# A macaron decoder layer: four instead of three of eight pairs by seven products in every other block of the gate and up groups

## Chip, core and metric

The kernel runs on one core of one Trainium2 chip. The metric is the device time of one execution in microseconds (us). Matrix products run on TensorE (PE), elementwise work on VectorE (DVE) and ScalarE (ACT), and loads of weights are issued on the queue of SyncE (SP).

## What is computed

One decoder layer on an input of 256 rows and 2048 columns: a half feed-forward network (FFN1), three gated token mixers, and a second half feed-forward network (FFN2). The change touches only the first product of the two FFNs:

```python
def swiglu_half_ffn(x, norm_g, w_gate_up, w_down):
    h = rmsnorm(x, norm_g)
    gate, up = jnp.split(h @ w_gate_up, 2, axis=-1)
    return 0.5 * ((jax.nn.silu(gate) * up) @ w_down)
```

`w_gate_up` has 2048 rows and 2 x 5632 columns, all in float32.

## The kernel before

**Precision.** A float32 operand is split into a high part that PE takes (`h`, `wh`) and the low rest (`l`, `wl`). A product is then three matmuls: high x high, low x high, high x low (`add_product`, L241). The split of a weight tile is called a cut (`cut`, L236): ACT copies the high part, DVE subtracts it from the raw weights to give the low part.

**Tiles.** The input is transposed once into eight pages, each with two k-tiles of 128 rows, both parts, and both row tiles (`t` = 0, 1). A pair `u` is two k-tiles, so there are eight pairs. The gate and up columns are worked off in eleven blocks of 512 columns (`NFC`). Block 0 goes through `mm_group`. Blocks 1 to 10 go through `pair_group` (L248), which computes 512 gate columns and 512 up columns for both row tiles at once: a 2 x 2 block of outputs (row tile `t`, half `n`).

**Two kinds of pair.** For each pair `pair_group` loads two 512 KB pieces of weights into a `raw` buffer (there are three). An ordinary pair has eight products: four outputs by two k-tiles, 24 matmuls with 128 x 512 outputs. Its cuts are two of 1024 elements per partition. A seven-product pair takes the 2 x 2 by 2 x 2 block product with seven multiplications (the scheme of Strassen and Winograd), 21 matmuls. For it the left side needs four combinations of the input, which `form_page` (L215) makes once per pair and FFN and keeps in a page of `forms`. The weights need combinations too, made anew in every block on DVE: `ta` (L290), `tb` (L295, L296), with a cut of each (`hal`, `hbl` are the low parts) beside a plain cut of 1024 and one of 512 elements. Its seven products go to three of the four output accumulators and to four intermediate ones, `p1`, `p5`, `p6`, `p7`. Each accumulator is one of the eight PSUM banks. After the last seven-product pair of a block, ACT copies `p1` and DVE makes four combinations of the intermediates (L314 to L318, tiles `ua`, `u`, `uv`). At the end of the block `ffn` adds them to the four accumulators (L471), and `gated` (L447) applies the gate (L453 on ACT, L455 on DVE).

**Order.** The order of pairs in a block is `MIXED`, (3, 0, 4, 1, 5, 2, 6, 7), and pairs 0, 1 and 2 are the seven-product ones, at the second, fourth and sixth place. `pair_group` takes its `seven` from the pages in `forms` unless it is given; `form_steps` makes three. The same function with the same order serves other weights (L595, L903, L925). The down product (L505, L511) uses it with orders of its own; in its second call five seven-product pairs alternate with ordinary ones.

**Side steps.** A queue `side` holds small steps that `tick` runs between matmuls. `pair_group` ticks twice in every ordinary pair that comes after the last seven-product pair of its block (L282), so four times in a block. `put` (L417) is two steps: each transposes half of the block's hidden values on PE, and the second one also writes them to DRAM on SP's queue (L431). The last block also takes `get` steps for the down product.

**Buffers and scheduling.** Cut weights have five buffers for each part (`wh`, `wl`). `ta`, `tb` and the parts of their cuts lie in a pool of 30 pages, which also holds the input's pages and the forms. A scheduler fixes the order of each engine's instructions when the kernel is built, and puts in the waits; loads on SP's queue are issued in that order.

Of the kernel before, what the change touches and what calls it, by code (L numbers as in the profile page):

```python
# [21 lines left out]
FF = 5632  # L22
NFC = FF // 512
DOWN = (2, 5, 8, 11, 14)
MIXED = (3, 0, 4, 1, 5, 2, 6, 7)
KF = FF // P
EPS = 1e-6
# [6 lines left out]
def hybrid_layer(  # L34
# [37 lines left out]
    side = deque()  # L72
# [139 lines left out]
    def lhs_of(tiles):  # L212
        return lambda k, part, t: tiles[k // 2][:, k % 2, part, t * P : (t + 1) * P]

    def form_page(forms, tiles, j):  # L215

        xp = tiles[j]
        v, f = temp([2, S], "fv"), temp([4, P], "ff")
        nc.vector.tensor_tensor(v, xp[:, :, 0, :].bitcast(F32), xp[:, :, 1, :].bitcast(F32), ALU.add)
        a12, a22, a11, a21 = (v[:, kk, t * P : (t + 1) * P] for kk in range(2) for t in range(T))  # L220
        nc.vector.tensor_tensor(f[:, 0, :], a21, a22, ALU.subtract)
        nc.vector.tensor_tensor(f[:, 1, :], f[:, 0, :], a11, ALU.subtract)
        nc.vector.tensor_tensor(f[:, 2, :], a11, a21, ALU.subtract)
        nc.vector.tensor_tensor(f[:, 3, :], f[:, 1, :], a12, ALU.add)
        dst = page([2, 4, P], F32R, "form")
        nc.scalar.activation(dst[:, 0, :, :], f, AF.Copy)
        nc.vector.tensor_tensor(dst[:, 1, :, :], f, dst[:, 0, :, :].bitcast(F32), ALU.subtract)
        forms[j] = dst
# [180 lines left out]
    def form_steps(forms, tiles, n=3):  # L409
        return [lambda j=j: form_page(forms, tiles, j) for j in range(n)]  # L410

    def ffn(lx, forms, rs, wgu, wd, stream, cb, before=None):
        hid, flat = [], {}
        hdram = dp.tile([NFC - 1, P, 4 * S], F32, tag="hd", name="hd", bufs=2)
        rh = st.tile([P, T], F32, tag="rh", name="rh")
# [1 line left out]
        def put(c, hd):  # L417

            dst = []

            def turn(jj):
                if jj == 0:
                    dst.append(page([4, S], F32, "hf"))
                ps = aux([2, S], "hid")
                for j in range(2):
                    for t in range(T):
                        k = 2 * jj + j
                        nc.tensor.transpose(ps[:, j, t * P : (t + 1) * P], hd[t][:, k * P : (k + 1) * P], ident)  # L428
                nc.scalar.activation(dst[0][:, 2 * jj : 2 * jj + 2, :], ps, AF.Copy)
                if jj == 1:  # L430
                    nc.sync.dma_start(out=hdram[c], in_=dst[0].rearrange("p k s -> p (k s)"))  # L431

            return [lambda: turn(0), lambda: turn(1)]
# [30 lines left out]
        for c in range(1, NFC):  # L464
            if c == NFC - 1:
                side.extend(put_last)
            acc, terms = pair_group(wgu, c * 512, FF + c * 512, lx, forms, MIXED)
            for n in range(2):
                for t in range(T):
                    d = terms[t, n]  # L470
                    nc.vector.tensor_tensor(d, acc[t, n], d, ALU.add)  # L471
            hd = gated(c, [terms[t, 0] for t in range(T)], [terms[t, 1] for t in range(T)])
            if c < NFC - 1:
                side.extend(put(c, hd))
            if c == NFC - 2:
                put_last = [lambda: get(0), lambda: get(1)]
        drain()
# [27 lines left out]
        ps, terms = pair_group(wd, 0, 512, lh, down, range(KF // 2), DOWN, first_block)  # L505
# [5 lines left out]
        ps, terms = pair_group(wd, 1024, 1536, lh, down, order, DOWN, second_block)  # L511
# [34 lines left out]
    forms0 = {}  # L546
# [3 lines left out]
    s0 = Stream([xv[:, :, c * 512 : (c + 1) * 512] for c in range(4)])  # L550
    cb, x1, rs, s1 = residual(s0, G_MIX, "x1")
    lx = lhs_of(x1)
    ffn(lhs_of(tiles0), forms0, rs0, ffn1_w_gate_up[0], ffn1_w_down[0], s0, cb, before=before)


    def head_norm(buf, nh, name):
# [378 lines left out]
        for t in range(T):  # L935
            nc.sync.dma_start(out=out[0, t * P : (t + 1) * P, c * 512 : (c + 1) * 512], in_=o[:, t, :])

    ffn(lhs_of(x2), forms2, rs, ffn2_w_gate_up[0], ffn2_w_down[0], s2, store)


# [30 lines left out]
```

## Time and profile before

| | us |
|---|---|
| median of 3 runs | 2128.67 (2128.15 to 2128.83) |
| profiled execution | 2128.03 |
| its span, first to last instruction | 2126.30 |
| PE busy | 2114.2 (99%) |
| DVE busy | 1739.4 (82%) |
| ACT busy | 1186.1 (56%) |

The span runs from the first instruction to the last on the core; the execution's time has some start and end around it. Blocks 1 to 10 of FFN1 lie between about 57 and 482 us of the span, those of FFN2 between about 1464 and 1889 us. Block 4 of FFN1 begins on PE at about 184.2 us and block 5 at 226.65 us. Ends of matmuls are modelled, so the start of one to the start of the next tells what it costs. The rows of DVE and ACT overlap with their neighbours by some hundredths to a tenth of a microsecond, so there too the distance of starts is the cost, where no idle time is noted.

### The profile page before, as it was taken

To read this page: it belongs to the slowest core of one execution; us is meant where nothing else is said; L and a number is where in the kernel's file an instruction comes from. 1 tells how busy PE (TensorE), PEld (TensorE's weight loads), DVE (VectorE), ACT (ScalarE), POOL (GpSimd) and SP (SyncE) were. 2 spreads that over 40 slices of the span, in tenths; PEclk is the share of its full clock that TensorE was granted. 3 is DMA by queue.
4 is the path that set the end of the run, shared out by engine and by line. 5 is a ranking of instruction groups with operands and counts; after the bars stand their busy time and mean duration, and the time that the engine had idled before them with its cause. 6 is when DMAs were issued, how large, how long until landed. Compare 5 with 4: busy or idle time off the path is not lost.

```text
span 2126.3 us, 26105 instructions
## 1 busy us (share of the span) xinstructions
PE 2114.2 (99%) x9683; PEld 1744.7 (82%) x9683; DVE 1739.4 (82%) x2221; ACT 1186.1 (56%) x1488; POOL 3.5 (0%) x24
## 2 busy tenths in 40 slices
PE   9999999999999999999999999999999999999999
PEld 7888888888888888887788888878888888888887
DVE  7898899889858788657669878898899889989675
ACT  6555555556545565555655555565555555556453
POOL 0000000000000000000000000000000000000000
PEclk9999999999999999999999999999999999999999
DMA  7666666666866654754456656575666666677764
GB/s 260 206 213 212 207 210 216 211 230 223 274 211 205 225 204 149 250 165 157 139 178 217 198 189 211 195 250 199 214 217 207 209 208 218 208 235 245 258 193 148
DMA packets 221508, 444.67 MB, mean 209 GB/s; under 512 B 12654, under 2 KB 13764, under 8 KB 221380
## 3 DMA queue, kind: packets, MB, share of 16 engines
q1 hardware_dynamic: 221088, 442.96, 62.7%
q8 instruction: 76, 1.25, 0.2%
q14 instruction: 52, 0.43, 0.1%
q10 hardware_dynamic: 292, 0.05, 0.0%
HBM read 426.16 MB, written 16.79 MB: 208 GB/s over the span
## 4 chain that ended last, share of the span: by engine, by line
PE 97%; DVE 1%; DMA 1%; ACT 0%; issue 0%; SPq 0%; ACTq 0%; DVEq 0%
PE mm L244 74%; PE mm L352 20%; PE hid L428 1%; DMA raw<-in_ffn_w_gate_up_dram 1%; DVE wl L346 0%; PE x L200 0%; DVE xr L389 0%; PE fpt L851 0%; PE fav L861 0%; PE mg L200 0%; PE flg L823 0%; PE mlg L729 0%; PE mav L756 0%; PE flg L821 0%; ACT wh L345 0%
## 5 line engine op out<-in xcount | busy, mean ns | idle before, releaser
L238 ACT ACTIVATE wh<-raw 128x1024 fp32r<-128x1024 f32 x608 | 599.7, 988 | 634.6 <-PE mm L244 362.5
L239 DVE TENSOR_TENSOR wl<-raw,wh 128x1024 fp32r<-128x1024 f32 x608 | 682.4, 1132 | 204.6 <-ACT wh L238 203.8
L244 PE MATMUL mm<-wh,x 128*128 128x512 f32 x2300 | 713.5, 391 | 0.0
L244 PEld LDWEIGHTS mm<-wh,x 128*128 128x128 f32 x2300 | 428.7, 188 | 87.3
L244 PE MATMUL mm<-wl,x 128*128 128x512 f32 x1150 | 446.7, 390 | 0.0
L244 PE MATMUL mm<-wh,hid 128*128 128x512 f32 x1168 | 357.7, 390 | 0.0
L352 PE MATMUL mm<-wh,x 128*128 128x512 f32 (+1 forms) x960 | 291.7, 382 | 2.9 <-ACT x L189 2.8
L346 DVE TENSOR_TENSOR wl<-raw,wh 128x1024 fp32r<-128x1024 f32 (+2 forms) x170 | 196.8, 1161 | 95.8 <-ACT wh L345 94.9
L345 ACT ACTIVATE wh<-raw 128x1024 fp32r<-128x1024 f32 (+2 forms) x170 | 170.5, 1009 | 169.7 <-PE mm L352 97.3
L244 PEld LDWEIGHTS mm<-wh,hid 128*128 128x128 f32 x1168 | 218.8, 188 | 45.1
L244 PEld LDWEIGHTS mm<-wl,x 128*128 128x128 f32 x1150 | 215.9, 188 | 45.3
L244 PE MATMUL mm<-wl,hid 128*128 128x512 f32 x584 | 222.4, 389 | 0.0
L352 PEld LDWEIGHTS mm<-wh,x 128*128 128x128 f32 x960 | 175.6, 188 | 38.6 <-ACT x L189 4.2
L352 PE MATMUL mm<-wl,x 128*128 128x512 f32 (+1 forms) x480 | 181.4, 379 | 0.2 <-DVE wl L346 0.2
L290 DVE TENSOR_TENSOR ta<-raw 128x1024 f32<-128x1024 f32 x101 | 123.1, 1219 | 12.0 <-DMA raw<-in_ffn_w_gate_up_dram 6.4
L244 PEld LDWEIGHTS mm<-wl,hid 128*128 128x128 f32 x584 | 109.6, 188 | 22.8
L239 DVE TENSOR_TENSOR hbl<-tb,hbh 128x1024 fp32r<-128x1024 f32 x101 | 123.2, 1220 | 2.5 <-ACT hbh L238 2.3
L239 DVE TENSOR_TENSOR hal<-ta,hah 128x1024 fp32r<-128x1024 f32 x101 | 123.2, 1220 | 1.4 <-ACT hah L238 1.4
L238 ACT ACTIVATE hbh<-tb 128x1024 fp32r<-128x1024 f32 x101 | 106.3, 1053 | 30.1 <-DVE tb L296 30.0
L238 ACT ACTIVATE hah<-ta 128x1024 fp32r<-128x1024 f32 x101 | 106.3, 1052 | 27.5 <-DVE ta L290 27.1
L244 PE MATMUL mm<-hah,form 128*128 128x512 f32 x404 | 121.5, 389 | 0.0
L352 PEld LDWEIGHTS mm<-wl,x 128*128 128x128 f32 x480 | 90.1, 188 | 16.3 <-DVE wl L346 0.6
(318 smaller groups left out, 2198.2 us busy)
## 6 DMA issues: line engine op xcount, KB each, us to landing
raw<-in_ffn_w_gate_up_dram SPq DMA_DIRECT2D x322, 512.0 KB, 4.5
raw<-in_ffn_w_down_dram SPq DMA_DIRECT2D x176, 512.0 KB, 5.1
raw<-in_w_in_dram SPq DMA_DIRECT2D x80, 512.0 KB, 5.1
raw<-in_w_in_dram SPq DMA_DIRECT2D x36, 1024.0 KB, 5.0
raw<-in_w_out_dram SPq DMA_DIRECT2D x32, 512.0 KB, 5.1
raw<-in_ffn_w_gate_up_dram SPq DMA_DIRECT2D x14, 1024.0 KB, 5.6
hd<-hf SPq DMA_DIRECT2D x20, 512.0 KB, 5.1
hg<-hd SPq DMA_DIRECT2D x20, 512.0 KB, 8.5
```

The lines of the kernel that those rows point to most:

```text
L238: nc.scalar.activation(dst[0], src, AF.Copy)
L239: nc.vector.tensor_tensor(dst[1], src, dst[0].bitcast(F32), ALU.subtract)
L244: nc.tensor.matmul(ps, sides[part], wt[i][:, col : col + 512], start=start and q == 0, stop=stop and q == 2)
L290: nc.vector.tensor_tensor(ta, s[:, 3:4, :].to_broadcast([P, 2, 512]), s[:, 1:3, :], ALU.add)
L345: nc.scalar.activation(hv, rv, AF.Copy)
L346: nc.vector.tensor_tensor(lv, rv, hv.bitcast(F32), ALU.subtract)
L352: nc.tensor.matmul(ps[t][i][:, :n], lhs(k, part, t), wt[:, kk, o : o + n], start=k == 0 and q == 0, stop=k == kt - 1 and q == 2,)
L428: nc.tensor.transpose(ps[:, j, t * P : (t + 1) * P], hd[t][:, k * P : (k + 1) * P], ident)
```

## The change

In both FFNs, blocks 3, 5, 7 and 9 (`more`) take the order `FOUR` in place of `MIXED` and have pairs 0 to 3 by seven products, at the first, third, fifth and seventh place. The other blocks keep three. A fourth page of `forms` is made by a side step that is queued at the end of block 1, behind the steps of `put`. `ffn` gets the list of input pages (`xt`) for it. In the blocks with `FOUR` only the last pair is ordinary and behind the last seven-product one, so these blocks tick twice.

```diff
--- before.py
+++ after.py
@@ -22,6 +22,7 @@
 FF = 5632
 NFC = FF // 512
 DOWN = (2, 5, 8, 11, 14)
+FOUR = (0, 4, 1, 5, 2, 6, 3, 7)
 MIXED = (3, 0, 4, 1, 5, 2, 6, 7)
 KF = FF // P
 EPS = 1e-6
@@ -409,7 +410,7 @@
     def form_steps(forms, tiles, n=3):
         return [lambda j=j: form_page(forms, tiles, j) for j in range(n)]
 
-    def ffn(lx, forms, rs, wgu, wd, stream, cb, before=None):
+    def ffn(lx, xt, forms, rs, wgu, wd, stream, cb, before=None):
         hid, flat = [], {}
         hdram = dp.tile([NFC - 1, P, 4 * S], F32, tag="hd", name="hd", bufs=2)
         rh = st.tile([P, T], F32, tag="rh", name="rh")
@@ -464,7 +465,10 @@
         for c in range(1, NFC):
             if c == NFC - 1:
                 side.extend(put_last)
-            acc, terms = pair_group(wgu, c * 512, FF + c * 512, lx, forms, MIXED)
+            more = c > 1 and c % 2 == 1
+            acc, terms = pair_group(
+                wgu, c * 512, FF + c * 512, lx, forms, FOUR if more else MIXED, range(4 if more else 3)
+            )
             for n in range(2):
                 for t in range(T):
                     d = terms[t, n]
@@ -472,6 +476,8 @@
             hd = gated(c, [terms[t, 0] for t in range(T)], [terms[t, 1] for t in range(T)])
             if c < NFC - 1:
                 side.extend(put(c, hd))
+            if c == 1:
+                side.append(lambda: form_page(forms, xt, 3))
             if c == NFC - 2:
                 put_last = [lambda: get(0), lambda: get(1)]
         drain()
@@ -550,7 +556,7 @@
     s0 = Stream([xv[:, :, c * 512 : (c + 1) * 512] for c in range(4)])
     cb, x1, rs, s1 = residual(s0, G_MIX, "x1")
     lx = lhs_of(x1)
-    ffn(lhs_of(tiles0), forms0, rs0, ffn1_w_gate_up[0], ffn1_w_down[0], s0, cb, before=before)
+    ffn(lhs_of(tiles0), tiles0, forms0, rs0, ffn1_w_gate_up[0], ffn1_w_down[0], s0, cb, before=before)
 
 
     def head_norm(buf, nh, name):
@@ -935,7 +941,7 @@
         for t in range(T):
             nc.sync.dma_start(out=out[0, t * P : (t + 1) * P, c * 512 : (c + 1) * 512], in_=o[:, t, :])
 
-    ffn(lhs_of(x2), forms2, rs, ffn2_w_gate_up[0], ffn2_w_down[0], s2, store)
+    ffn(lhs_of(x2), x2, forms2, rs, ffn2_w_gate_up[0], ffn2_w_down[0], s2, store)
 
 
 # ---- launch: one core; inputs and outputs as the reference has them ----
```

## Rows read from the trace of the kernel before

**Rows 1.** engine totals on the page, and the chain that ended last, by engine

```profile
PE 2114.2 (99%) x9683; PEld 1744.7 (82%) x9683; DVE 1739.4 (82%) x2221; ACT 1186.1 (56%) x1488; POOL 3.5 (0%) x24
...
PE 97%; DVE 1%; DMA 1%; ACT 0%; issue 0%; SPq 0%; ACTq 0%; DVEq 0%
```

**Rows 2.** PE's waits over the span: who waited for whom, us in total, times, longest

```profile
PE mm L352 <- ACT x L189: 2.8, 2, 1.4
```

**Rows 3.** the chain in order of time: start us, us, what (blocks 4, 5; FFN2)

```profile
178.90 38.79 PE mm L244 x171
221.34 38.79 PE mm L244 x171
...
1628.06 38.82 PE mm L244 x171
```

**Rows 4.** stretches: PE, PEld, DVE, ACT, POOL busy us (instructions), PEclk, DMA share, GB/s

```profile
182.30:224.90 42.60, 42.60 (x194) 35.26 (x193) 37.64 (x42) 24.37 (x28) 0.00 (x0) 1.00 0.63 211
640.00:680.00 40.00, 40.00 (x178) 33.15 (x177) 36.30 (x39) 23.74 (x26) 0.00 (x0) 1.00 0.62 208
1930.00:1970.00 40.00, 40.00 (x180) 33.16 (x179) 38.34 (x51) 25.59 (x32) 0.00 (x0) 1.00 0.69 226
```

**Rows 5.** PE in time, blocks 4 and 5: start us, us, engine, line, operation

```profile
203.24 0.61 PE L244 MATMUL mm<-hbh,form 128*128 128x512 f32 x2
...
217.53 0.27 PE L428 MATMUL hid<-ident,u 128*128 128x128 f32 x1
...
226.65 0.62 PE L244 MATMUL mm<-wh,x 128*128 128x512 f32 x2
```

**Rows 6.** groups by line: names, shapes, xcount | busy us, mean ns | idle before

```profile
L227 DVE TENSOR_TENSOR form<-ff,form 128x512 fp32r<-128x512 f32 x22 | 14.8, 685 | 1.6 <-ACT form L226 1.6
...
L221 DVE TENSOR_TENSOR ff<-fv 128x128 f32<-128x128 f32 x22 | 6.2, 284 | 0.2
```

**Rows 7.** DVE in time, blocks 3 and 4: start us, us, engine, line, operation

```profile
172.49 1.22 DVE L239 TENSOR_TENSOR wl<-raw,wh 128x1024 fp32r<-128x1024 f32 x1
...
180.89 0.68 DVE L471 TENSOR_TENSOR ua<-mm,ua 128x512 f32<-128x512 f32 x1
...
182.09 0.68 DVE L471 TENSOR_TENSOR u<-mm,u 128x512 f32<-128x512 f32 x1
...
183.29 0.68 DVE L471 TENSOR_TENSOR u<-mm,u 128x512 f32<-128x512 f32 x1
183.89 1.22 DVE L239 TENSOR_TENSOR hbl<-tb,hbh 128x1024 fp32r<-128x1024 f32 x1
...
186.16 0.68 DVE L471 TENSOR_TENSOR uv<-mm,uv 128x512 f32<-128x512 f32 x1
186.76 0.74 DVE L455 SCALAR_TENSOR_TENSOR u<-u,rh,ua 128x512 f32<-128x512 f32 x1
187.42 1.22 DVE L239 TENSOR_TENSOR wl<-raw,wh 128x1024 fp32r<-128x1024 f32 x1
...
189.22 1.22 DVE L239 TENSOR_TENSOR wl<-raw,wh 128x1024 fp32r<-128x1024 f32 x1
190.35 1.22 DVE L239 TENSOR_TENSOR hal<-ta,hah 128x1024 fp32r<-128x1024 f32 x1
...
195.65 1.22 DVE L239 TENSOR_TENSOR hbl<-tb,hbh 128x1024 fp32r<-128x1024 f32 x1
...
202.91 0.69 DVE L296 TENSOR_TENSOR tb<-tb,raw 128x512 f32<-128x512 f32 x1
...
214.32 0.69 DVE L315 TENSOR_TENSOR u<-mm,ua 128x512 f32<-128x512 f32 x1 [0.51 <-PE mm L244]
```

**Rows 8.** waits from 97.2 to 479.9, nine blocks of FFN1 (columns of rows 2)

```profile
ACT wh L238 <- PE mm L244: 82.0, 76, 2.0
...
DVE ta L290 <- DMA raw<-in_ffn_w_gate_up_dram: 2.1, 5, 0.9
```

**Rows 9.** waits of SP's DMA queue from 97 to 480 (columns of rows 2)

```profile
SPq L431 <- ACT hf L429: 7.4, 9, 2.0
```

## Prediction

> **What bounds the kernel now.** I read the page's engine totals first. TensorE (PE) is busy 99% of the span, VectorE (DVE) 82%, and the chain that ended last is 97% PE [rows 1]. Busy time alone proves little, since the ends of matmuls are modelled, so the second view is PE's own waits: there are eight in the whole trace, 7.5 us together, the largest group of two is in the row, and none stands in the gate and up groups [rows 2]. Third, the chain in order of time. A block of a gate and up group there is one unbroken piece of 171 matmuls in 38.79 us, or 0.2268 us each, and the next block's piece starts 42.44 us later. FFN2 shows the same (38.82 us) [rows 3]. So a block costs its number of matmuls times 0.2268 us: three pairs of 21 and five of 24 make 183, or 41.5 us, and eight transposes for `put`, the first of which is in [rows 5], bring the rest. PE is the bound, at a fixed pitch, and nothing else ends a wait there.
>
> DVE is close behind. In a block of 42.6 us it is busy 37.64 us [rows 4], and that is where a change of this kind can fail.
>
> **What it removes.** An ordinary pair issues 24 matmuls of 512 columns (4 outputs x 2 k-tiles x 3 terms), a seven-product pair 21. Blocks 3, 5, 7 and 9 of two FFNs get one more seven-product pair each: 8 x 3 = 24 matmuls less, and their weight loads. At 0.2268 us that is 5.44 us. All of it lies on the path, as the chain runs through every one of these matmuls. Transposes, evictions and loads keep their number.
>
> The row has a rival price. The Trainium skill, TensorE: Matmul & The Clock Gate, Back-to-back issue gap, gives a warm isolated gap of N/2.4 + 2.5 ns, that is 216 ns for 512 columns; the trace does not agree, since its pitch is 227 ns in these blocks. By the page the saving would be 24 x 0.216 = 5.18 us, a quarter of a microsecond less.
>
> **What it adds to DVE.** The rows of DVE in order of time give the pitch of instructions that follow each other without a gap: 1.13 us for 1024 elements (189.22 to 190.35), 0.60 for 512 (183.29 to 183.89), 0.66 for the gating (186.76 to 187.42) [rows 7]. An ordinary pair has two of 1024, 2.27 us. A seven-product pair has four of 1024 (plain low part, `ta`, `hal`, `hbl`) and three of 512, 6.34 us. One swapped pair adds 4.07 us to a block. A block now takes 3 x 6.34 + 5 x 2.27 + 6.1 (four `u`/`uv` combinations and four adds of 0.60, two gatings) = 36.5 us of DVE; a block of the new kind takes 40.6 us, against a PE time of 42.44 - 0.68 = 41.8 us. On its own that is tight, but the new blocks alternate with old ones: 36.5 + 40.6 = 77.1 us in 84.2 us, 92%.
>
> DVE is not perfectly dense even when it has work. From 172.49 to the end of the `tb` at 202.91 it issues 17 instructions of 1024, 16 of 512 and 2 gatings, 30.2 us of pitch in 31.0 us [rows 7], so it delivers 97%. 92% then becomes 94%, and a new block alone becomes 41.7 of 41.8 us. Two stretches show PE unhurt at such loads: 640 to 680 us, in the second down block, where five seven-product pairs alternate with ordinary ones, has DVE at 36.30 of 40 us; 1930 to 1970 has 38.34 of 40. In both PE is busy for all 40 us [rows 4].
>
> **How much lead there is.** The low part `hbl` of the second seven-product pair starts at 195.65 and is done 1.22 us later; the product that reads it starts at 203.24 [rows 5, 7]. That lead, 6.4 us, is among the smallest in the block, and it is not set by DVE's speed alone: ScalarE (ACT) waits 82 us in nine blocks for matmuls to free its cut buffers [rows 8], so cutting is held back by PE. Where a new block follows an old one, one ordinary pair fewer lies between the last seven-product pair and the next. Between them now: three ordinary pairs and a seven, 3 x 5.44 + 4.76 + 0.8 of transposes = 21.9 us of PE, and 3 x 2.27 + 6.34 + 6.1 = 19.3 us of DVE, 2.6 us over. After: 16.4 against 17.0, 0.6 us short. The lead falls by 3.2 us, to some 3.2 us, and the alternation behind it gives back 10.2 - 8.6 = 1.6 us a couple. The new block's end has the same distance (ordinary, ordinary, seven), so the same dip. Cover remains, but half of it goes; were it gone, each microsecond of dip would be a microsecond of PE idle, eight or sixteen times.
>
> **The rest.** The fourth `form_page` costs DVE two instructions of 512 and four of 128, at most 2 x 0.685 + 4 x 0.285 = 2.5 us [rows 6], and ACT one, once per FFN, in block 2. DVE has 42.4 - 36.5 = 5.9 us over there, and its page is read only by the seventh pair of block 3, some 30 us later: nothing on the path. Were the cover gone, 2 x 2.5 = 5 us would cancel the gain. It keeps one more of 30 pages: 8 of the input and 4 of forms leave 18, three sets of the six that a seven-product pair uses, and a pair's set is free again 10.2 us later, when the second next is cut: nothing, with rival two as its upper bound.
>
> The new blocks have two side steps instead of four, in the last pair. `put` needs both and gets both, but its second transposes move to the block's end. The hidden write that SyncE (SP) issues behind them stands ahead of weight loads on its queue. Today that write waits 7.4 us in nine blocks, 2.0 us at most [rows 9], and DVE waits 2.1 us for weights in all [rows 8]. I bound it at 0 to 2.0 us a block; it eats lead, not PE time, and I take 0 because the loads run up to three raw buffers ahead. The last block and `put_last` keep their order.
>
> **Sum.** The profiled execution took 2128.03 us (span 2126.30): 2128.03 - 5.44 = 2122.6. The median of the runs is 0.64 us higher, which gives 2123.2. I take 2122.9.
>
> **The rivals.**
>
> *One: DVE's lead does not carry over (partial loss).* If every new block runs at DVE's pace, it takes the 41.7 us above and about 0.5 us of waits in DVE's order, as the 0.51 us that the first combination waits for PE at 214.32 [rows 7], 42.2 us instead of 41.8: 0.4 x 8 = 3.2 us lost, 2126. For it: a new block alone fills DVE. Against it: the two-block load of 94%, and the second down block.
>
> *Two: the banks run out at the head of a new block (slower).* A seven-product pair opens seven of the eight PSUM banks within its first 4.1 us; an ordinary pair opens four. The first four can be those of the four intermediate products, freed long before. The fifth is wanted 2.7 us after the start, the sixth at 3.4, the seventh at 4.1, and they come from the add of each accumulator of the block before. A block begins at 226.65 [rows 5] and, one period earlier, at 184.2; around it the adds start at 180.89, 182.09, 183.29 and 186.16 [rows 7] and end 2.6, 1.4 and 0.2 us before the start and 2.6 us after. The smallest margin is 4.1 + 0.2 = 4.3 us. Now the last add already stands behind one `hbl` and one `ta` on DVE, and the order of DVE's queue is the scheduler's. If a whole seven-product pair's cuts (6.34 us) come ahead of the third add, PE stalls 2.0 us at each head: 8 x 2.0 - 5.4 = +10.9 us, 2139. It decides from the point where the head stalls over 0.68 us. For it: this head occurs nowhere in the trace before. Against it: 4.3 us of margin, and adds ranked ahead of later cuts in the program. The Trainium skill, Perfetto Trace Analysis, Optimization Strategy, says that the same gap repeated on the engine that should be saturated can mean too little PSUM for the next tile; the trace before has no such gap, and by that rule this rival's gap would show at the head of every new block.
>
> *Three: it does less than it says.* Excluded by the count: the four forms are ready and the order has them, so 9683 matmuls become 9659.
>
> **How the numbers follow.** Forecast (5.44 us saved, under 1.2 us of stalls): 0.62, its own range 2121.8 to 2124.4. Rival one, 2124.4 to 2128.5: 0.23. Rival two, and form or load cover gone past the gain: 0.14. 0.01 for a gain of more than 5.44 us. About 0.2% (4.3 us, so 2124.4 and 2132.9) is what a measurement of this kernel can tell from no change: faster 0.62, same 0.24, slower 0.14. The range takes in the forecast and rival one: 2121.5 to 2128.5.
>
> **What would show it.** Right: 9659 matmuls; new blocks 41.8 us from start to start and old ones 42.4; no PE wait in the blocks; DVE above 41 us in new blocks; ACT's waits for matmuls clearly under 82 us. Wrong: PE idle at the start of blocks 3, 5, 7 and 9 with an add as releaser (rival two), or inside them with a cut `wl`, `hal` or `hbl` as releaser (rival one), or a pitch other than 0.2268 us.

## The result and the profile after

The changed kernel takes 2132.62 us (median of 20 executions, 2129.31 to 2135.42) against 2128.76 us before (20 on the same chip): a ratio of 1.0019, 95% interval 1.0012 to 1.0025. It is 3.9 us slower where a saving of 5.4 us was forecast, and it lies above the range of 2121.5 to 2128.5.

The profiled execution is the quickest of the twenty (2129.31 us, span 2127.6 against 2126.3 before, mean granted clock 1.000), so its trace shows only 1.3 us of the 3.9. Of the others eleven list a mean clock of 0.999 (median 2131.9) and eight 0.998 (median 2134.0). The trace explains the 1.3 us, and shows where the 5.4 us of saving went.

The totals and the chain on the page, after:

```profile
PE 2113.5 (99%) x9659; PEld 1741.0 (82%) x9659; DVE 1769.2 (83%) x2273; ACT 1197.9 (56%) x1506; POOL 3.5 (0%) x24
...
PE 95%; DVE 2%; DMA 1%; ACT 1%; issue 0%; SPq 0%; ACTq 0%; DVEq 0%
```

Against [rows 1] there are 24 matmuls fewer and 52 DVE instructions more: 8 pairs with seven DVE instructions in place of two, and 12 for the two form pages. DVE, DMA and ACT now stand in the chain with 4%.

PE's waits, after (who waited for whom: us in total, times, longest). Neither group exists before [rows 2]:

```profile
PE mm L245 <- DVE form L228: 1.9, 2, 1.0
PE mm L245 <- ACT form L227: 1.6, 2, 1.0
```

A form written where? PE in order of time gives the place. First before, then after (start us, us, engine, line, operation):

```profile
469.26 0.39 PE L244 MATMUL mm<-hbl,x 128*128 128x512 f32 x1
...
481.33 0.84 PE L244 MATMUL mm<-wh,hid 128*128 128x512 f32 x3
...
716.79 0.39 PE L352 MATMUL mm<-wh,x 128*128 128x512 f32 x1
...
1888.07 1.29 PE L244 MATMUL mm<-wh,hid 128*128 128x512 f32 x5
...
2121.37 0.39 PE L244 MATMUL mm<-wl,hid 128*128 128x512 f32 x1
```

```profile
475.01 0.39 PE L245 MATMUL mm<-hbl,x 128*128 128x512 f32 x1
...
478.90 0.61 PE L245 MATMUL mm<-wh,hid 128*128 128x512 f32 x2
...
494.62 0.50 PE L245 MATMUL mm<-wh,form 128*128 128x512 f32 x1 [0.60 <-ACT form L227]
...
496.83 0.50 PE L245 MATMUL mm<-wh,form 128*128 128x512 f32 x1 [0.96 <-DVE form L228]
...
717.52 0.39 PE L353 MATMUL mm<-wh,x 128*128 128x512 f32 x1
...
1885.37 0.61 PE L245 MATMUL mm<-wh,hid 128*128 128x512 f32 x2
```

The matmuls on `hid` begin the down product, and those on L352 (after: L353) follow FFN1's. FFN1's down product begins 481.33 - 478.90 = 2.43 us earlier, FFN2's 2.70 us. 12 matmuls x 0.2268 us are 2.72 us per FFN: the gate and up groups give nearly what was computed (2.21 and 2.67 us, counted from the last matmul of block 0), with hardly a wait in them. Then FFN1's down product takes 717.52 - 478.90 = 238.62 us in place of 235.46, 3.16 us longer; FFN2's, whose last matmul starts at 2122.29 and not at 2121.37, is 3.62 us longer. The saving is given back where one product hands over to the next. The part between FFN1's down product and the end of FFN2's block 0 comes out 0.76 us shorter, and the end behind FFN2's last matmul 0.36 us longer: -2.43 + 3.16 - 0.76 - 2.67 + 3.62 + 0.36 = 1.28 us.

The chain around the handover, before and then after (start us, us, what):

```profile
477.87 22.21 PE mm L244 x98
```

```profile
477.93 12.93 PE mm L245 x57
...
492.49 1.21 DVE wl L240
...
496.18 0.61 DVE form L228
...
496.83 3.24 PE mm L245 x13
```

Before, PE alone carries it. After, the chain leaves PE at 490.86 for DVE's cuts and the down product's first form. Why is DVE late there? DVE in order of time, after:

```profile
475.21 0.69 DVE L316 TENSOR_TENSOR u<-mm,ua 128x512 f32<-128x512 f32 x1 [3.08 <-PE mm L245]
...
488.35 0.68 DVE L475 TENSOR_TENSOR uv<-mm,uv 128x512 f32<-128x512 f32 x1
...
491.83 0.74 DVE L456 SCALAR_TENSOR_TENSOR uv<-uv,rh,u 128x512 f32<-128x512 f32 x1
...
496.10 0.68 DVE L228 TENSOR_TENSOR form<-ff,form 128x512 fp32r<-128x512 f32 x1
```

DVE first idles 3.08 us for the last seven-product pair of block 10, then has everything at once: combinations, adds until 488.35, the last gating at 491.83, the form at 496.10. So just ahead of the handover it is not DVE that lacks time; PE delivers its input late. The pair itself is late: its last `hbl` matmul starts 3.9 us ahead of the down product; before, 12.1 us. PE's program, as the scheduler ordered it, shows the same: between the last matmul that reads a form and the down product there are 59 others before (transposes counted) and 18 after, and the matmuls that read a form, from FFN1's block 1 to the down product, lie in 30 unbroken runs before and in 126 after. The scheduler has torn the seven-product pairs apart and put ordinary products between their matmuls. This text calls such an order torn. In it the blocks stay free of waits.

### The profile page after: what moved, and what is told of

It is laid out like the page before. It is cut to its first block, busy times and chain, and to the rows that moved or that the text cites. A ratio compares the mean times of both kernels' runs of the same rounds, so it can differ in the third digit from the quotient of the medians.

```text
span 2127.6 us, 26074 instructions
## 1 busy us (share of the span) xinstructions
PE 2113.5 (99%) x9659; PEld 1741.0 (82%) x9659; DVE 1769.2 (83%) x2273; ACT 1197.9 (56%) x1506; POOL 3.5 (0%) x24
## 4 chain that ended last, share of the span: by engine, by line
PE 95%; DVE 2%; DMA 1%; ACT 1%; issue 0%; SPq 0%; ACTq 0%; DVEq 0%
PE mm L245 71%; PE mm L353 21%; PE hid L429 1%; DVE wl L240 1%; DMA raw<-in_ffn_w_gate_up_dram 1%; PE x L201 0%; DMA raw<-in_ffn_w_down_dram 0%; ACT wh L239 0%; DMA raw<-in_w_mem_kv_dram 0%; DVE wl L347 0%; DVE ta L291 0%; PE fpt L857 0%; DVE xr L390 0%; PE fav L867 0%; PE mg L201 0%
## 5 line engine op out<-in xcount | busy, mean ns | idle before, releaser
L240 DVE TENSOR_TENSOR wl<-raw,wh 128x1024 fp32r<-128x1024 f32 x608 | 674.6, 1123 | 158.8 <-ACT wh L239 153.9
L245 PE MATMUL mm<-wh,x 128*128 128x512 f32 x2204 | 675.8, 391 | 0.2 <-ACT hf L430 0.2
L245 PEld LDWEIGHTS mm<-wh,x 128*128 128x128 f32 x2204 | 411.7, 188 | 84.8 <-ACT hf L430 0.6
L245 PE MATMUL mm<-wl,x 128*128 128x512 f32 x1102 | 414.3, 390 | 0.0
L353 PE MATMUL mm<-wh,x 128*128 128x512 f32 (+1 forms) x960 | 292.3, 383 | 0.7 <-ACT x L190 0.6
L245 PEld LDWEIGHTS mm<-wl,x 128*128 128x128 f32 x1102 | 206.9, 188 | 43.2
L353 PEld LDWEIGHTS mm<-wh,x 128*128 128x128 f32 x960 | 176.2, 189 | 36.1 <-issue 2.9
L353 PE MATMUL mm<-wl,x 128*128 128x512 f32 (+1 forms) x480 | 181.9, 380 | 0.0
L239 ACT ACTIVATE hbh<-tb 128x1024 fp32r<-128x1024 f32 x109 | 114.9, 1054 | 73.5 <-DVE tb L297 72.9
L240 DVE TENSOR_TENSOR hal<-ta,hah 128x1024 fp32r<-128x1024 f32 x109 | 132.8, 1219 | 11.5 <-ACT hah L239 11.5
L291 DVE TENSOR_TENSOR ta<-raw 128x1024 f32<-128x1024 f32 x109 | 132.7, 1217 | 11.4 <-DMA raw<-in_ffn_w_down_dram 6.9
L239 ACT ACTIVATE hah<-ta 128x1024 fp32r<-128x1024 f32 x109 | 114.6, 1051 | 43.9 <-DVE ta L291 43.8
L240 DVE TENSOR_TENSOR hbl<-tb,hbh 128x1024 fp32r<-128x1024 f32 x109 | 132.8, 1219 | 7.2 <-ACT hbh L239 7.1
L353 PEld LDWEIGHTS mm<-wl,x 128*128 128x128 f32 x480 | 90.5, 189 | 16.1 <-issue 0.3
```

The source lines that it names most:

```text
L239: nc.scalar.activation(dst[0], src, AF.Copy)
L240: nc.vector.tensor_tensor(dst[1], src, dst[0].bitcast(F32), ALU.subtract)
L245: nc.tensor.matmul(ps, sides[part], wt[i][:, col : col + 512], start=start and q == 0, stop=stop and q == 2)
L291: nc.vector.tensor_tensor(ta, s[:, 3:4, :].to_broadcast([P, 2, 512]), s[:, 1:3, :], ALU.add)
L353: nc.tensor.matmul(ps[t][i][:, :n], lhs(k, part, t), wt[:, kk, o : o + n], start=k == 0 and q == 0, stop=k == kt - 1 and q == 2,)
```

## The experiments

In the expectations of the first runs, theory one says that the loss sits at the handover, where the plan of block 10, behind new block 9, is torn; theory two says that it comes from the load of all the new blocks. Theory three, and theory A of the later runs, say that DVE falls behind in each new block and carries this lateness on. "Longer down products" is worked out as above, FFN1 / FFN2, from each run's profile; "distance" is the number of matmuls between the last one that reads a form and the down product (59 before, 18 with the change). Each ratio is to the kernel before on the same chip.

### Which new block it takes

```diff
-            more = c > 1 and c % 2 == 1
+            more = c in (3, 5, 7)      # e_no9
+            more = c == 9              # e_only9
```

> The change without block 9: only blocks 3, 5 and 7 of both FFNs have four seven-product pairs, so 18 matmuls fewer than before instead of 24 (18 x 0.2268 = 4.1 us). Theory one (handover): the loss is made where block 10, which follows a block of the new kind directly, hands over to the down product; there PE's planned order puts the last seven-product pair's matmuls 18 matmuls ahead of the block's end instead of 59, so the combinations, the adds and the first form page of the down product come late. Here a plain block 8 and 9 stand between, and the planned order has 59 again. Theory one expects 2126.3 - 4.1 = 2122.2 us of span, about 2124.6 by the runs, no wait for a form in the down product, granted clock 1.00. Theory two (DVE is too full in every new block, and that costs time or clock in the blocks themselves): three quarters of the loss stays, about 2131.5 by the runs and waits of PE in blocks 3 to 8.

> Only block 9 of both FFNs has four seven-product pairs: 6 matmuls fewer, 1.4 us. PE's planned order at the end of block 10 has the last seven-product matmuls 25 matmuls ahead of the end. Theory one (handover): almost the whole loss of the change is here: 2 x 3.1 us of PE waits at the start of the down products and the lower clock behind them, so about 2128.8 - 1.4 + 6 + 3 = 2136, at least over 2131. Theory two (fullness of DVE in every new block): a quarter of the change's loss, 2128.8 + 1 = 2129.8 or less.

Without block 9: 2125.96 us, ratio 0.9987 (0.9978 to 0.9996); down products 0 / 0 us longer, distance 59. Block 9 alone: 2132.06, ratio 1.0016 (1.0007 to 1.0025); 2.56 / 2.58 us longer, distance 25. The longest of PE's waits that is new in e_only9 stands there, once per FFN:

```profile
PE mm L245 <- ACT hbh L239: 1.9, 2, 1.0
```

One new block next to the handover suffices for most of the loss. This spoke for theory one.

```diff
-                ... FOUR if more else MIXED, range(4 if more else 3)
+                ... FOUR if more else MIXED, range(3)      # e_order3
```

> The order of pairs of the change in blocks 3, 5, 7 and 9, but with three seven-product pairs (0, 1, 2 at the first, third and fifth place) as before; the fourth form page is made and not used. No matmul fewer. Theory one: no loss, 2128.8 within 0.1% (the planned order at the end of block 10 has 59 matmuls as before). A rival in which a block that begins with a seven-product pair, or two side steps instead of four, costs by itself: over 2131 here, with PE waits at the heads of blocks 3, 5, 7 and 9.

The order `FOUR` with three seven-product pairs takes 2128.26, ratio 0.9998 (0.9989 to 1.0007), span +0.3 us. Order and the two missing ticks cost nothing, nor does the fourth page, which is made and kept here without being used; it takes the fourth pair to lose.

### The order fixed everywhere

If the torn plan alone did it, keeping PE's matmuls of blocks 2 to 10 in the order of the code should give the gain.

```diff
-            nc.tensor.matmul(
+            one = nc.tensor.matmul(
                 ps, sides[part], wt[i][:, col : col + 512], start=start and q == 0, stop=stop and q == 2
             )
+            if pin[0]:
+                tc.keep_in_program_order(one)
...
+            pin[0] = c > 1             # e_pinpe, ahead of pair_group; False behind the last block
```

> The change as it is, with PE's matmuls of blocks 2 to 10 held to program order, so that each pair's products stay together and the last seven-product pair of block 10 ends 59 matmuls ahead of its end, as before. The scheduler's view of DVE's fullness stays what it is. Theory one (the torn order at the handover is what costs): 5.4 us saved, span 2121, about 2123.3 by the runs. Theory two (DVE is really too late): the matmuls that the scheduler had put later now wait for their cuts, PE idles in the new blocks with a cut as releaser, 1 us a block or more, so over 2128.

2136.35 us, ratio 1.0034 (1.0022 to 1.0045). Theory one's 2123.3 fell. The down products are 0 us longer, and PE waits in the blocks, as theory two had it, though not by 1 us in each. PE's waits of e_pinpe, and its one long wait of FFN1 in order of time:

```profile
PE mm L246 <- DVE hbl L241: 7.2, 8, 3.0
```

```profile
148.49 0.50 PE L246 MATMUL mm<-hbl,form 128*128 128x512 f32 x1 [2.96 <-DVE hbl L241]
```

DVE ahead of it:

```profile
129.07 0.69 DVE L319 TENSOR_TENSOR u<-mm,ua 128x512 f32<-128x512 f32 x1 [0.51 <-PE mm L246]
...
132.86 0.68 DVE L221 TENSOR_TENSOR fv<-x 128x512 f32<-128x512 f32 x1
...
137.69 0.69 DVE L229 TENSOR_TENSOR form<-ff,form 128x512 fp32r<-128x512 f32 x1
...
147.22 1.22 DVE L241 TENSOR_TENSOR hbl<-tb,hbh 128x1024 fp32r<-128x1024 f32 x1
```

From the first combination of block 2 to block 3's first `hbl` DVE works 18.15 us with one hole of 0.33, and its `hbl` comes 3 us too late. The six instructions of the fourth form page lie in this stretch (132.86 to 137.69) and take 0.60 + 0.94 + 0.60 = 2.1 us by their pitch. Blocks 5, 7 and 9 wait 0.21 each; no head of an ordinary block behind them waits. So DVE is short at these places. The kernel before, built with the same pin, is the same program on every engine (it was not run): its order was the code's already, and the code's order costs it nothing.

### The page elsewhere

```diff
-    def form_steps(forms, tiles, n=3):
+    def form_steps(forms, tiles, n=4):         # 3 for the mixers
...
-            if c == 1:
-                side.append(lambda: form_page(forms, xt, 3))
```

f_early_pin has this and the pin, f_early this alone.

> PE's matmuls of blocks 2 to 10 in program order, as in the run that held them, and the fourth form page made ahead of block 1 instead of at the end of block 2. Theory one says that the 3 us for which PE waits in block 3 come from the form page's six DVE instructions (2.0 us) and their ACT copy between the combinations of block 2 and the first cuts of block 3: it falls to under 1 us, the other new blocks keep some 0.3 us each, and the time is about 2128.6 - 5.4 + 2.5 = 2125.7. If the head of the first new block is too tight by itself, the wait stays at 2 us or more and the time over 2130.

> The change with the fourth form page made ahead of block 1 instead of in block 2, nothing held to program order. PE's planned order at the end of block 10 stays as in the change (18 matmuls). Theory one: the wait at the handover stays, 2132 as with the change, within 1 us. If the form page in block 2 were the root of the torn order, 2126 or less.

f_early_pin: 2128.17, ratio 0.9996 (0.9987 to 1.0004), down products 0 us longer. The waits are as small as was expected, the time is 2.5 us over the 2125.7. PE's waits in it, and the first of them in order of time:

```profile
PE mm L246 <- DVE hbl L241: 1.7, 8, 0.2
```

```profile
155.58 0.61 PE L246 MATMUL mm<-hbh,form 128*128 128x512 f32 x2
156.41 0.50 PE L246 MATMUL mm<-hbl,form 128*128 128x512 f32 x1 [0.21 <-DVE hbl L241]
156.75 0.63 PE L246 MATMUL mm<-hbh,x 128*128 128x512 f32 x2
```

The wait of 2.96 us in block 3's first pair is gone; what is left is 0.2 us in the second pair of each new block, so the page was 2.75 us a FFN. By the starts of the matmuls each of these waits costs more than its 0.21 us: three matmuls take 156.75 - 155.58 = 1.17 us in place of 0.68, so 0.49, and 2.0 us in four blocks.

f_early: 2127.97, ratio 0.9997 (0.9988 to 1.0006), down products 1.24 / 1.73 us longer, with a distance of 18 in FFN1, as in the change, and 24 in FFN2. Neither expectation, 2132 or 2126, came: without the page in block 2 the plan is as torn, and the handover costs 1.9 us less per FFN. So the distance does not set the size of the loss. And the two runs, which differ by the pin alone, take the same time: with PE's order fixed the blocks lose 2.0 us per FFN, with the order free the handover loses 1.24 and 1.73. Here the torn order moves the loss.

Three lighter variants ask the same. g_nopage leaves the fourth page out, and pair 3 reads pair 2's. g_light leaves out the low part `hbl` of the first pair of each new block, one DVE instruction of 1.13 us, and uses `hal` in its place. g_odd_b1 makes the page in block 1's first pair.

```diff
+                forms[3] = forms[2]                                       # g_nopage
+            hb = (hb[0], ha[1])   # if order is FOUR and i == 0           # g_light
+        side.append(lambda: form_page(forms, xt, 3))  # ahead of block 1, early=c == 1   # g_odd_b1
```

> The change with the fourth form page left out: pair 3 takes the page of pair 2 instead, so this part of the product is not the reference's; every other instruction is the change's. It takes DVE's 2.0 us and one ACT copy out of block 2, once per FFN. Theory three (a DVE debt: in each new block DVE falls short at the head, the page in block 2 adds 2.0 us, and what is not paid there is carried to the handover) expects the wait at the start of the two down products to fall from 6.8 us together to 2 or 3, and the time from 2132.6 to 2128 within 1 us, as with the page made early. Theory one (only the torn order at the end of block 10 counts, which is planned at 24 matmuls here against 18) expects 2131 to 2132.6.

> The change, but the first seven-product pair of each new block makes no low part of its second combination (no hbl, one DVE instruction of 1.13 us) and uses another low part in its place, so its products are not the reference's; matmuls, pages and order of pairs are the change's, the planned order at the end of block 10 has 23 matmuls. Theory three (DVE debt) expects 4 x 1.13 = 4.5 us less DVE per FFN at exactly the heads, more than the whole debt of some 3.2 us: no wait or under 1 us at the handovers, 5.4 us saved, 2123.5 to 2126. Theory one expects 2131 or more, as the order at the handover stays torn.

> The change with the fourth form page made in the first pair of block 1, where DVE waits for buffers anyway, instead of at the end of block 2; blocks 3, 5, 7 and 9 as in the change. Theory three: as without the page, 2128 within 1.5 us, since the heads' own debt of 4 x 0.3 us a FFN and the tight handover remain. A rival (the page costs wherever it stands): 2132.

g_nopage: 2128.85, ratio 1.0001 (0.9992 to 1.001), 2.27 / 2.01 us longer. g_light: 2128.31, ratio 0.9998 (0.9989 to 1.0007), 1.65 / 1.64. g_odd_b1: 2126.62, ratio 0.9992 (0.9984 to 1.0001), 1.66 / 1.64. Each takes one to two microseconds off 3.16 / 3.62, none takes all. g_light was expected at 2123.5 to 2126 by theory three and at 2131 or more by theory one: both missed, and the loss is larger than one cut a block.

### The order fixed from some block on

If DVE is late through the blocks and the torn order only hides it, the lateness must appear wherever the order is fixed. The pin of e_pinpe, from another block on:

```diff
+            pin[0] = c == NFC - 1      # f_pin10
+            pin[0] = c >= NFC - 2      # h_pin9
+        pin[0] = True                  # h_pindown: the down product's first call alone
```

> The change with PE's matmuls held to program order in block 10 alone, the last block of the gate and up groups; the blocks before it keep the planned, torn order. The last seven-product pair then ends 59 matmuls ahead of the down product, not 18. Theory one (what costs is the late end of that pair at the handover): no wait for a form or for a hidden page in the down product, gate and up groups save what they did, about 2128.6 - 5.4 + 1 = 2124. Theory two (cuts of block 10 are late in earnest, since DVE carries a backlog out of block 9): PE waits inside block 10 for a cut, 2 to 3 us in each FFN, and the time is 2129 or more.

> TensorE's matmuls of blocks 9 and 10 stay in the order in which the program writes them; blocks 1 to 8 are free to be interleaved. Theory A (a debt of VectorE that is carried from block to block: the interleaved order of the earlier blocks hides late cuts until the order is fixed): PE waits 2 to 5 us per FFN within the first products of block 9 (for an add, so for a PSUM bank, or for hbl), under 1.5 us at block 10, and 0 at the down product; 2128 to 2133 us. Theory B (the interleaving of block 10 alone makes the loss, with no debt before it): no wait over 0.6 us at block 9 or 10 and none at the down product; 2123.5 to 2126 us.

> Only the first block of the down product keeps the program's order on TensorE; the gate and up blocks are planned as in the change (last seven-product matmul 18 matmuls ahead of the down product). If the loss comes from late adds, gatings and forms behind the torn end of block 10, the down products still lose 2 to 4 us each and the time is 2130 to 2135 us. If it comes from the down product's own interleaving, its loss falls under 1 us each: 2126 to 2129 us.

2132.05 (ratio 1.002, 1.0011 to 1.003), 2137.78 (1.0046, 1.0029 to 1.0062) and 2146.09 (1.008, 1.0065 to 1.0095). PE's waits, each twice, once per FFN: of f_pin10 in the first pairs of block 10, of h_pin9 in the first pair of block 9, of h_pindown at the down product's first seven-product pair:

```profile
PE mm L246 <- DVE u L479: 4.3, 2, 2.1
```

```profile
PE mm L246 <- DVE u L479: 7.5, 2, 3.8
```

```profile
PE mm L246 <- ACT hah L240: 13.9, 2, 7.0
```

With block 10 or 9 fixed the down product is 0 us longer and the stall is at that block's head. It is for an add, not for a cut as f_pin10's theory two had it. Theory A of h_pin9 holds for the waits (its total of 2133 was passed, see the clock below), and h_pindown missed both of its expectations: with that call fixed, PE can't put its ordinary pairs first, and 7 us show. DVE ahead of h_pin9's stall, and PE's end of it:

```profile
395.54 0.68 DVE L479 TENSOR_TENSOR u<-mm,u 128x512 f32<-128x512 f32 x1
...
399.01 1.21 DVE L241 TENSOR_TENSOR hal<-ta,hah 128x1024 fp32r<-128x1024 f32 x1
...
402.01 0.68 DVE L479 TENSOR_TENSOR u<-mm,u 128x512 f32<-128x512 f32 x1
```

```profile
402.74 0.73 PE L246 MATMUL mm<-hbh,x 128*128 128x512 f32 x2 [3.77 <-DVE u L479]
```

Between the second add (395.54) and the third (402.01) stand cuts and weight combinations above all, 4.6 us by their pitch, and PE waits 3.77 us for the bank. By the Trainium skill, Perfetto Trace Analysis, Optimization Strategy, a gap that repeats on the engine that should be saturated can mean too little PSUM for the next tile; here, with one such gap in each FFN, the banks are too few because the adds that free them are late. Why are they late? From the last matmul of block 8's last seven-product pair to block 9's first `hah` matmul, first in h_pin9 and then in f_early_pin, where block 8 is fixed too:

```profile
389.04 0.40 PE L246 MATMUL mm<-hbl,x 128*128 128x512 f32 x1
...
395.54 0.61 PE L246 MATMUL mm<-hah,form 128*128 128x512 f32 x2
```

```profile
384.14 0.39 PE L246 MATMUL mm<-hbl,x 128*128 128x512 f32 x1
...
397.58 0.62 PE L246 MATMUL mm<-hah,form 128*128 128x512 f32 x2
```

The torn order of block 8 leaves DVE 6.5 us for the combinations and adds in place of 13.4, and f_early_pin has no wait at this place. So the stall at the first fixed block shows what the torn order ahead of it had put off, and not what a new block costs DVE by itself.

How long does the lateness last? The version without block 9, fixed from block 8 on (behind new block 7), and from block 9 on (one ordinary block later):

```diff
-            more = c > 1 and c % 2 == 1
+            more = c in (3, 5, 7)
+            pin[0] = c >= 8            # j_no9_pin8;  c >= 9: j_no9_pin9
```

> Blocks 3, 5 and 7 alone have four seven-product pairs (9 is ordinary), and TensorE's matmuls of blocks 8, 9 and 10 keep the program's order. Theory A (a debt of VectorE, hidden by the interleaving and carried out of each new block): as the first pinned block follows a new one, PE waits 1.5 to 3 us at the head of block 8 in each FFN, for an add, as block 10 did in f_pin10; 2128 to 2132 us. Theory B (the loss belongs to block 9 next to the handover alone): no wait over 0.6 us at block 8; 2124 to 2126.5 us.

> As the last, but pinned from block 9 on, behind one whole ordinary block. If one ordinary block pays the debt back, PE waits under 0.6 us at block 9's head and nothing later: 2124 to 2127 us. If it does not, the wait at block 9's head is as long as at block 8's in the other run, less some 1 us: 2127 to 2131 us.

2133.33 (ratio 1.0022, 1.0011 to 1.0033; 2132 at most was expected) and 2130.8 (1.0014, 1.0002 to 1.0025). PE's waits in the first two pairs of block 8, and in those of block 9:

```profile
PE mm L246 <- DVE u L479: 4.3, 2, 2.1
...
PE mm L246 <- DVE u L321: 0.7, 2, 0.4
```

```profile
PE mm L246 <- DVE u L479: 3.5, 2, 1.7
```

Fixed from the ordinary block behind a new one, PE stalls there for 2.1 + 0.4 = 2.5 us (f_pin10 shows 2.1 + 0.5 behind block 9); fixed from one ordinary block later, for 1.7. Theory A holds for the torn plan: its lateness outlasts the new block, and one ordinary block does not remove it. That every new block leaves DVE 2.5 us late is not shown: in e_pinpe and f_early_pin, fixed from block 2 on, the heads of blocks 4, 6, 8 and 10 behind the same new blocks have no wait. Without block 9 three ordinary blocks follow, and the handover is free.

### Versions without a new block next to the handover

```diff
-            more = c > 1 and c % 2 == 1
+            more = c in (2, 4, 6, 8)   # f_even, g_even_b1, h_even_late
+            more = c in (2, 4, 6)      # h_247
```

f_even and h_247 make the page ahead of block 1 as f_early, g_even_b1 as g_odd_b1, h_even_late in the side steps of block 1 (`side.append` ahead of the loop).

> Four seven-product pairs in blocks 2, 4, 6 and 8 instead of 3, 5, 7 and 9, with the fourth form page made beside the other three ahead of block 1. The same 24 matmuls fewer. A plain block 9 lies between the last new block and block 10, whose last seven-product pair is planned to end 50 matmuls ahead of the down product. Theory one (handover): 5.4 us saved, at most 1 to 2 us lost in the mixers' planning as without block 9, so 2123.3 to 2125.5. Theory two (a new block costs wherever it stands): 2130 or more.

> Four seven-product pairs in blocks 2, 4, 6 and 8, the fourth form page made in the first pair of block 1. A plain block 9 ahead of block 10 lets DVE catch up before the handover. Expected: 5.4 us saved in the gate and up groups, no wait at the handovers, 2123.3 if the mixers' planned order costs nothing more, 2125.4 if it costs the 2.1 us that it did with the page made ahead of block 1. Theory one: the last seven-product pair is planned to end 32 matmuls ahead of the down product, so some wait there, 2126 or more.

> Blocks 2, 4, 6 and 8 have four seven-product pairs in place of 3, 5, 7 and 9, and the fourth page is made by a side step in block 1, so that nothing is added ahead of block 1. The planned order has the last seven-product matmul 50 matmuls ahead of the down product. Theory (a loss only where that distance is short, and early pages cost 2.5 us ahead of block 1): down products cost 0, no 2.5 us ahead of block 1, page made beside block 1: 2122.5 to 2125.5 us. If the page's place matters more than the distance (it then falls in the last 20 us before block 2's first seven-product pair): a wait for form or hbl in block 2, 2126 to 2130 us.

> Blocks 2, 4 and 6 alone have four seven-product pairs (18 matmuls less, 4.08 us), the fourth page made ahead of block 1. Planned distance of the last seven-product matmul 59, as in the kernel before. Theory: no loss at the down products, 2.5 us ahead of block 1 for the first FFN, so 2128.8 - 4.1 + 2.5 = 2127.2 at most and 2125 if a part of the page is hidden; the mixers' plan adds -1 to +2.5 us, as in all kernels so far.

f_even: 2125.35, ratio 0.9984 (0.9975 to 0.9993), 0 us longer, distance 50. h_even_late: 2124.26, ratio 0.9982 (0.9972 to 0.9991), 1.07 / 0.27 us longer where 0 was expected, distance 50. h_247: 2126.78, ratio 0.9992 (0.9982 to 1.0001), 0 us longer, distance 59. g_even_b1: 2129.11, ratio 1.0003 (0.9994 to 1.0013), 2.57 / 2.58 us longer, distance 32. h_even_late has 9659 matmuls, as the change, and the chain at its handover is PE's again:

```profile
477.87 22.21 PE mm L245 x98
```

It beats both kernels, 4.5 us under the one before; f_even can't be told from it. g_even_b1 has the same new blocks and loses at the handover, as theory one had it for a distance of 32; so an ordinary block 9 does not suffice by itself, and where the page goes alters the plan to its end. Over all kernels in which PE's order is free, a distance of 50 or more went with at most 1.1 us there, one of 32 or less with 1.2 to 3.6 us per FFN. The two go together; which comes first in the planner was not tried.

## Why the prediction was wrong

**Saving: right.** 9659 matmuls, and 2.21 and 2.67 us less in the gate and up groups of 2.72 each, with no wait over 0.2 us in the blocks. These signs of being right came; they all look inside the blocks. One reading of [rows 2] was loose: two of the eight waits stand in block 0 of FFN1, none in blocks 1 to 10, which is what the sum needs.

**DVE's cost: right, and not the sum that decides.** 52 instructions were counted, 52 came. Block 3 (new) and block 4 (ordinary), after (columns of [rows 4]):

```profile
141.70:183.50 41.80, 41.78 (x189) 34.18 (x187) 36.94 (x40) 24.29 (x29) 0.00 (x0) 1.00 0.66 222
183.50:226.00 42.50, 42.35 (x190) 35.06 (x191) 40.41 (x48) 25.74 (x30) 0.00 (x0) 1.00 0.59 200
```

36.94 + 40.41 = 77.35 us of DVE in 84.3 us, against 77.1 in 84.2 computed. So close an agreement is partly luck: the computed sum goes by starts, and the same column had 2 x 37.64 = 75.3 us before [rows 4] where 73.0 were computed. And the sign that was asked for, over 41 us in the new block, came out the other way round: the new block has less than the ordinary one behind it, which carries work that the new block left undone. The prediction read from 92% that the lead carries over; an average over two blocks can't say that.

**The lead: the step that failed.** The sum has no stall in it because "Cover remains, but half of it goes": a lead of 6.4 us, less a dip of 3.2. The dip was about right, the lead that it was taken from was not there. In f_early_pin, with PE's order fixed and the page made ahead of block 1, DVE and PE at the second seven-product pair of block 2, which lies ahead of every new block:

```profile
113.57 1.23 DVE L241 TENSOR_TENSOR wl<-raw,wh 128x1024 fp32r<-128x1024 f32 x1 [1.72 <-ACT wh L240]
114.72 1.22 DVE L241 TENSOR_TENSOR hbl<-tb,hbh 128x1024 fp32r<-128x1024 f32 x1
```

```profile
119.03 0.39 PE L246 MATMUL mm<-hbl,form 128*128 128x512 f32 x1
```

`hbl` is done 119.03 - 115.94 = 3.1 us ahead of the matmul that reads it. At the same place before it was 6.8 (0.45 more than the prediction's 6.4, which went by the row ahead of that matmul). DVE even idles 1.72 us there, for ACT's part of a cut that was put ahead of `hbl`. In e_pinpe block 2 still has its 6.8, but the ordinary blocks 4, 6 and 8 reach 3.1 us at most: the lead is not regained between two new blocks. Why the planned order of the cuts keeps it at 3.1 stays open. The second pair of new block 3 in f_early_pin then falls from 3.1 us of cover to 0.2 of waiting, by 3.3 us. The prediction took the plan of the kernel before as given. Its "each microsecond of dip would be a microsecond of PE idle" stands under a condition, the cover gone, that was held not to occur.

**Rival one: right where the order is fixed.** Its sign, PE idle inside a new block with `hbl` as releaser, is what f_early_pin shows in all eight, 0.49 us each by starts, 3.9 us together where 3.2 were priced. In the change itself, where the order is free, it does not show in the blocks.

**The form page: "nothing on the path" failed.** The 5.9 us that DVE has over in block 2 are a sum over that block, but the page is put between block 2's combinations and block 3's `hbl`, where none is over. Its price for the case that was held not to occur ("Were the cover gone, 2 x 2.5 = 5 us would cancel the gain") is what e_pinpe and f_early_pin measure: 2.96 - 0.2 = 2.75 us per FFN. Against f_early it is 3.16 - 1.24 = 1.9 and 3.62 - 1.73 = 1.9 us of the handover. By itself, without the fourth pair, it cost nothing (e_order3).

**Rival two, and the place.** Its sentence, a pair's cuts ahead of the third add, is nearly the order of h_pin9 (4.6 us of cuts in place of 6.34), with 3.8 us of stall in place of the 2.0 computed, behind a block that was torn. In the change itself no head stalls, because PE's order is the scheduler's too. The prediction left DVE's order to the scheduler and took PE's as given. With PE's order free the loss stands at the start of the down product, a place that the prediction did not look at: 3.16 and 3.62 us, with block 9 alone (e_only9) 2.56 and 2.58, with the other three (e_no9) none. That ordinary products are moved forward until none are left to move fits these runs. It does not account for all: e_only9 loses 2.56 us for one new block, where with PE's order fixed a new block costs 0.49. How the loss of the change divides between DVE's shortage and the torn plan stays open.

**`put` and the loads: size wrong, result right.** Waits in nine blocks, after (columns of [rows 2]; the last from SP's queue):

```profile
ACT wh L239 <- DMA raw<-in_ffn_w_gate_up_dram: 48.2, 23, 5.3
ACT wh L239 <- PE mm L245: 45.9, 48, 2.6
...
SPq L432 <- ACT hf L430: 34.3, 7, 8.1
```

SP's write waits 34.3 us in place of 7.4 [rows 9], past the bound of 2.0 a block, and ACT, which never waited for weights [rows 8], now does so for 48.2 us. Its waits for matmuls fall from 82.0 to 45.9 as forecast. But h_even_late, the fastest, shows 47.4 us in the first of these groups too, so this wait alone is not what costs.

**What stays open.** 2.6 us of the 3.9 are not in the trace, as only the quickest execution was profiled. One cause can be seen in other kernels. Granted clock is the first of the last three columns; in j_no9_pin8 behind the same stall of 2.1 us in FFN1 and in FFN2:

```profile
366.00:368.00 2.00, 2.00 (x6) 1.54 (x6) 2.00 (x4) 0.00 (x0) 0.00 (x0) 0.51 0.03 8
1776.00:1778.00 2.00, 2.00 (x10) 1.64 (x9) 2.00 (x3) 1.06 (x1) 0.00 (x0) 1.00 0.00 0
```

In FFN1 PE runs 6 matmuls in 2 us at 1.2 GHz, in FFN2 10 at 2.4 GHz. The gate and up groups are 3.3 us longer than before in the one and 1.1 in the other, so the fall costs some 2 us on top of the stall. The change's handover waits may bring such falls in most executions; that is argued and not shown. The Trainium skill, TensorE: Matmul & The Clock Gate, What's actually happening, has the clock set by how busy PE has been of late, in two states; 0.51 and 1.00 agree with the two states. Why one and the same stall is followed by the one here and by the other there, no run shows. Nor is it explained why the time between the two FFNs' blocks moves by -0.8 to 2.6 us with edits that don't touch it.

## What to carry to other kernels

Weigh work added to the second-busiest engine at the tightest place, from the last matmul that it needs to the first that needs it, and count there everything that a scheduler may put between (adds, gatings, side steps); an average over a block says little. Take care with a lead that was read in the old plan: here the new plan did not keep it. Where a scheduler may reorder the bounding engine, a shortage can show not where it arises but at a later place where the order can't give way, so look at the handover to the next product. Fix the order through all blocks to see what the shortage costs; an order that is fixed only from some block on also shows what the plan ahead of it has put off. Here the swap paid where an ordinary block lay between the last new one and block 10 and the one-time work was done in block 1 (h_even_late).

## What the hardware showed that was not expected

A stall of PE of 2 us cost about twice its length in one place: behind it the granted clock was 0.51 in one FFN (366 us) and 1.00 in the other (1776 us), in the same execution, with the same stall. A wait of 0.21 us cost 0.49 by the starts of the matmuls around it. And in the change no wait of PE is over 0.2 us for ten blocks, and then 3 us are lost in one place.
